# A fp32 encoder trunk on one core: the weights' low parts by an accumulating DMA in place of a VectorE subtraction

## The chip, the cores and the metric

The kernel runs on one NeuronCore of a Trainium2 chip. The core has a matrix engine (TensorE, PE in the profile, with its weight loads as PEld), three engines that work element by element (VectorE, DVE; ScalarE, ACT; GpSimd, POOL), an engine that only issues and waits (SyncE, SP), and 16 DMA engines that all queues share. The metric is the device time of one launch in microseconds. Beside the times stand profiled executions, whose span runs from the first to the last instruction of the program.

## The reference

Two layers of a mixer block work on x of 512 tokens by 1024 channels, in float32. In each layer the normalised input goes through one wide projection; its columns feed a gated convolution module, a bidirectional retention of four heads, and a windowed attention of 16 heads over 4 key heads. Each branch has an output projection, the three are merged by sigmoid gates, and a last projection returns to the residual stream.

```
h = rms_norm(x, norm_g)
z = h @ w_in                                   # 1024 x 14848
...
y_conv = conv_module(...) @ w_conv_out         # 1024 x 1024
y_ret  = retention_branch(...) @ w_ret_out     # 2048 x 1024
y_attn = window_attention_branch(...) @ w_attn_out
g = sigmoid(g_logit + b_gate)
merged = g0 * y_conv + g1 * y_ret + g2 * y_attn
return x + merged @ w_out
```

Every weight is used once per launch, and all 512 tokens are in the core at once.

## The kernel before

**Products in two parts.** TensorE multiplies in a shorter format (float32r) than float32. So each operand is split into a high part, the value rounded to that format, and a low part, the value less the high part, and a product a·b is three matmuls: high·high, high·low and low·high (`mm3`, line 407). An operand's split is `hilo`, a ScalarE copy that rounds and a VectorE subtraction; the weights are split in `weights` (line 387).

**Weights.** The host cuts all matrices into 312 tiles of 128 partitions by 1024 columns (512 KB), 156 for each layer, in the order in which they are used. For each tile SyncE's queue issues a load into `raw` (tag `wraw`), ScalarE writes `wh`, the rounded copy, and VectorE writes `wl`, raw less wh. The tags `wraw`, `wh` and `wl` have three buffers each (`POOLS`, line 27). A buffer of `raw` is free again when `wl` is written, a buffer of `wh` or `wl` when the last matmul that reads it is done.

```
nc.sync.dma_start(out=raw, in_=self.io["wpk"][i])
nc.scalar.copy(out=wh, in_=raw)
nc.vector.tensor_tensor(out=wl, in0=raw, in1=wh.bitcast(F32), op=ALU.subtract)
```

**What uses a tile.** `columns` takes 128 output columns from one tile: eight blocks of 128 rows, three matmuls of 512 tokens each, 24 matmuls into one bank of PSUM (tag `pc`, three banks). `tokens` (line 428) takes four tiles for 512 columns, with tokens on the partitions, in four banks (tag `ps`); each tile feeds 24 matmuls. `tokens256` (line 438) makes a group of four heads' queries from two tiles; for each of four blocks of tokens it goes through all of the first tile and then all of the second (12 matmuls of 256 columns each), so both tiles are held until the last block. There are four such pairs in each layer.

**Order.** The program is first recorded and then put in order by a planner (`Plan`, `order` at line 241), which plays the instructions through with a price for each. Each engine takes, whenever it is free, the most urgent instruction whose operands are there and whose tile has a buffer. Urgency is the place in the program plus an offset; a weight tile's load has the offset -20 us (`LOAD_EARLY`), its split -16 us (`SPLIT_EARLY`), and buffers of one tag are given out in program order. The result is a fixed order on each engine and queue; on the chip an engine that waits holds up what stands behind it. All instructions of the plan are issued from one line, so the profile gives them all line 318 and tells them apart by the tiles' names. The planner's price of a DMA is 60 ns for the queue that issues it, its bytes at 350 GB/s one transfer after the other, and 2 us more until it has landed.

**Stages.** A layer goes through four retention heads (with the convolution's projections and its 31 taps, a VectorE chain in the background, between their steps), then the convolution's layer norm and the keys and values, then the attention, between whose steps gates and projections are set out (`ATT_FILL`), and at the end two projections in sequence (`finish`). GpSimd has little to do before: 62 instructions, memsets, small powers for the norms, and a copy of the attention's sinks into the tiles of the scores.

Of the kernel before, what the change touches and what calls it, by code (L numbers as in the profile page):

```python
# [25 lines left out]
# room, in tiles  # L26
POOLS = {"big": 15, "pp": 8, "mid": 3, "th": 2, "wide": 2, "pads": 1, "wraw": 3, "wh": 3, "wl": 3}
PSUM_POOLS = {"pc": 3, "ps": 4, "ps1": 1}
# planned for: the wait between engines, in ns, and how much longer than its price an instruction takes
LATENCY = 350  # L30
MARGIN = {"vector": 1.06, "scalar": 1.06}
# urgency, in ns
# [3 lines left out]
# the order of the attention's gates (A), merge gates (G), queries (Q) and the convolution's projection (C) between its steps  # L36
ATT_FILL = ["C0", "C1 Q1", "C2", "C3", "C4", "C5 Q2", "C6", "C7", "A0 G0", "Q3 A1", "A2 G1", "A3 G2", "G3", "A4 G4", "A5 G5", "G6", "G7", "A6 A7"]

# columns of the combined input projection
# [4 lines left out]
# columns of the packed parameters  # L44
# [3 lines left out]
# columns of the packed constants  # L48
# [5 lines left out]
class View:  # L54
    """A part of a tile that is allocated when its first instruction is issued.

    ix holds the numbers of the elements that it covers, with the partitions in two halves."""
# [27 lines left out]
    def reshape(self, *shape):  # L85
        """Free dimensions split or joined in order."""
        old = self.ix.shape[1:]
        names = "abcdefgh"
        ix = self.ix.reshape(self.ix.shape[0], *shape)
        fine = len(old) <= len(shape)  # L90
        many, few = (shape, old) if fine else (old, shape)
        groups, i = [], 0
        for n in few:
            g, m = [], 1
            while m < n or (not g):
                m *= many[i]
                g.append(names[i])
                i += 1
            groups.append("(" + " ".join(g) + ")")
        flat = " ".join(names[:len(many)])  # L100
        pat = f"p {' '.join(groups)} -> p {flat}" if fine else f"p {flat} -> p {' '.join(groups)}"
        return self._then("rearrange", (pat, dict(zip(names, many))), ix)
# [42 lines left out]
class Plan:  # L145
    """Records the instructions, orders them, and issues them to Tile in that order.

    Every engine takes, whenever it is free, the most urgent of the instructions whose operands are
    there and whose tiles have room; the engines take turns at a bank of PSUM. Urgency is the place in the program, in ns of the tensor
    engine's work, and an offset. Tiles with one tag are given room in the order of the program, so  # L150
    an order always exists."""
# [16 lines left out]
    def cost(self, engine, method, kw):  # L168
        out = kw.get("out")
        n = out.size if isinstance(out, View) else 0  # L170
        if method == "dma_start":
            return 60
        if engine == "tensor":
            if method == "transpose":
                return 107
            f32 = kw["rhs"].tile.dt == F32
            return max(n, 256 if n > 1 else 64) * (4 if f32 and n > 1 else 1) / 2.4
        src = kw.get("in0", kw.get("in_"))
        psum = isinstance(src, View) and src.tile.tag.pool.psum
        scalars = sum(isinstance(kw.get(k), View) for k in ("scalar", "scalar1", "scalar2", "scale", "bias"))  # L180
        if engine == "scalar":
            return (52 if psum else 94) + 0.833 * n + 93 * (scalars + (kw.get("accum_out") is not None))
        if engine == "gpsimd":
            if kw.get("op") == ALU.pow:
                return 290 + 166 * n
            return 75 + 2.25 * n
        if method in ("bn_stats", "tensor_reduce"):
            n = src.size
        if method == "reciprocal":
            return 62 + 8 * n  # L190
        if method in ("tensor_scalar", "tensor_copy", "memset"):
            n = n or kw["ap"].size
            return 68 + n * (1.042 if psum else 0.521) + 61 * scalars
        if method == "tensor_tensor_reduce":
            return 130 + 1.04 * n
        return 69 + 1.042 * n + 61 * scalars

    def record(self, engine, method, kw):
# [8 lines left out]
        for writes, v in sorted(views, key=lambda x: x[0]):  # L207
            t = v.tile
            tiles[id(t)] = t
            ix = v.ix.ravel()  # L210
            # a start of accumulation clears the whole bank's marks: it comes behind what the bank holds
            seen = t.writer if writes and engine == "tensor" else t.writer[ix]
            deps.update(np.unique(seen).tolist())
            if writes:
                mask = np.zeros(t.writer.size, bool)
                mask[ix] = True
                for r, m in t.readers:
                    if r != number and (m & mask).any():
                        deps.add(r)
                t.writer[ix] = number  # L220
                t.readers = [(r, m) for r, m in t.readers if (m & ~mask).any()]
            else:
                mask = np.zeros(t.writer.size, bool)
                mask[ix] = True
                t.readers.append((number, mask))
# [15 lines left out]
    def order(self):  # L241
# [12 lines left out]
        while len(result) < len(ops):  # L254
# [4 lines left out]
            for e in names:  # L259
# [3 lines left out]
                if free[e] <= t:  # L263
# [15 lines left out]
                    if item is not None:  # L279
# [10 lines left out]
                        if op.method == "dma_start":  # L290
                            n = max(v.size for v in op.args.values() if isinstance(v, View))
                            dma_free = max(dma_free, t) + n * P * 4 / 350
                            op.end = dma_free + 2000
# [39 lines left out]
class Pair:  # L333
    """A [128, 8, 512] array in two tiles of four rows each."""
# [8 lines left out]
class Builder:  # L343
# [43 lines left out]
    def weights(self, key):  # L387
# [7 lines left out]
        with nc.urgency(SPLIT_EARLY):  # L395
            nc.scalar.copy(out=wh, in_=raw)
            nc.vector.tensor_tensor(out=wl, in0=raw, in1=wh.bitcast(F32), op=ALU.subtract)
        return wh, wl

# [4 lines left out]
    def mm3(self, out, a, b, start, stop):  # L404
        """out (+)= (ah + al)^T (bh + bl), without al^T bl."""
        (ah, al), (bh, bl) = a, b
        self.mm(out, ah, bh, start, False)
        self.mm(out, ah, bl, False, False)
        self.mm(out, al, bh, False, stop)

    def columns(self, key, src, pool="pc"):
        """128 columns of src @ w, channels on partitions."""
# [10 lines left out]
    def rows(self, p, t, k, w, c):  # L423
        """adds the part of row k to 128 tokens' columns of src @ w_in."""
# [3 lines left out]
    def tokens(self, col):  # L428
        """512 columns of src @ w_in with tokens on partitions."""
# [8 lines left out]
    def tokens256(self, col):  # L438
        """256 columns of src @ w_in with tokens on partitions, two blocks of tokens in a bank."""
# [20 lines left out]
    def silu2(self, out, p):  # L460
        """2 silu(p) = (1 + tanh(p / 2)) p"""
# [6 lines left out]
    def rstd_of(self, acc, diag):  # L468
        """acc: [128, 512] sums of squares, to be added over the partitions."""
# [41 lines left out]
    def new_input(self, l):  # L511
        """Room for a layer's input, scaled by the norm's gain and split."""
        self.ng = self.gains[:, l * NK:(l + 1) * NK]
        self.uh = self.pair(F32R)
        self.ul = self.pair(F32R)
        self.acc = self.pp()

    def take(self, k):
        """x[k]: x[k] * g split, and its squares into the running sum."""
# [32 lines left out]
    def normalise(self):  # L552
        """h = RMSNorm(x), split."""
# [13 lines left out]
    def derive(self):  # L567
# [6 lines left out]
        # lg[:, 0:4] = log gamma forward; lg[:, 4:8] = -log gamma backward  # L574
# [17 lines left out]
    def toeplitz(self, h):  # L592
        """decay by distance: gamma_f^d for d >= 0, gamma_b^-d for d < 0."""
# [11 lines left out]
    def conv_in(self, c):  # L605
        """a * 2 sigmoid(b) into the padded rows, then the taps in the background."""
# [17 lines left out]
    def queries(self, h, cos, sin):  # L624
        """q, k: channels on partitions; rotary, split."""
# [7 lines left out]
    def values(self, h, first):  # L633
        """v: tokens on partitions; split."""
# [9 lines left out]
    def head(self, h, first):  # L644
# [13 lines left out]
        # scores, transposed: keys on partitions  # L658
# [11 lines left out]
        # gate  # L670
# [3 lines left out]
        # P v  # L674
# [21 lines left out]
        # back to channels on partitions, gated, split  # L696
# [10 lines left out]
        # output projection of two heads  # L707
# [19 lines left out]
    def gate_tanh(self, out, branch, m):  # L727
        """tanh(g / 2) of a merge gate: 2 sigmoid(g) = 1 + tanh(g / 2)"""
# [10 lines left out]
    def conv_stats(self):  # L739
        """y - mean in place, and 1/std spread over the partitions."""  # L740
# [59 lines left out]
    def qk_norm(self, pt, gain):  # L800
        """RMS norm over each head's 64 channels and rotary; tokens on partitions."""
# [29 lines left out]
    def transposes(self, qn, c):  # L831
        """heads 2c and 2c + 1 of four: [128 tokens, (t, h), 64] -> [128, tokens]."""
# [21 lines left out]
    def k_transposes(self):  # L854
        """keys with the channels twice on the partitions, high and low parts."""
# [11 lines left out]
    def q_transposes(self):  # L867
        """queries with the high parts of the channels on the lower partitions, the low parts on the upper."""
# [221 lines left out]
```

## Time and profile before

| | |
|---|---|
| runs | 2034.23 and 2035.17 us, median 2034.7 |
| profiled execution, span | 2032.9 us |
| matmuls and transposes on TensorE | 9436 |
| DMA moved | 184.29 MB, 91 GB/s over the span |
| weight loads | 312 of 512 KB, 3.5 us from issue to landing (median) |
| VectorE's subtractions for the weights | 312, 1222 ns each |
| ScalarE's casts of the weights | 312, 1050 ns each |

The span of the profiled execution is 1.8 us under the median of the runs. In the profile's groups a line names the engine, the operation, what it writes and reads by the tiles' names (`wl<-wraw,wh`), the shapes and the count; behind the bar stand the busy time in microseconds, the mean of one instruction in nanoseconds, and the idle time of the engine just before, with what ended it. A wait stands as who waited, for whom, the total in microseconds, how often, and the longest. A line of the timeline begins with the start and the length of what it merges, in microseconds; "x3" means three instructions in a row. A line of the table by stage begins with a stretch of the span and gives, for each engine, its busy time and its number of instructions, then the granted clock, the busy share of the DMA engines, and GB/s.

### The profile page before, as it was taken

How to read it: one execution, taken by the hardware profiler on the slowest of the kernel's cores; microseconds unless marked ns; L12 is line 12 of the kernel's file. 1: busy time of each engine (PE TensorE's matmuls, PEld its weight loads, DVE VectorE, ACT ScalarE, POOL GpSimd, SP SyncE). 2: the span in 40 equal slices, each digit the busy share in tenths (PEclk: the TensorE clock that was granted, in tenths of full speed). 3: DMA queues.
4: the chain of work that ended last, by engine and by line, in shares of the span. 5: the costliest groups of instructions: out<-in, count | busy, mean ns of one | idle time of the engine just before them, and what ended most of it. 6: DMA issues, size and time to landing. Idle time of an engine off the chain costs nothing.

```text
span 2032.9 us, 24260 instructions
## 1 busy us (share of the span) xinstructions
PE 2021.1 (99%) x9436; PEld 1661.8 (82%) x9436; DVE 1425.8 (70%) x2254; ACT 834.9 (41%) x1361; POOL 56.9 (3%) x62
## 2 busy tenths in 40 slices
PE   8999999999999999999999999999999999999999
PEld 6888888888788888888888888888888888888887
DVE  8788887588575556665567888875885755576652
ACT  5323223233344556673332332232333445566731
POOL 0000000000000000000000000000000000000000
PEclk9999999999999999999999999999999999999999
DMA  5322232222232222223432222222222322222232
GB/s 214 101 73 92 82 94 92 70 86 67 89 94 94 81 75 73 63 82 121 166 99 91 83 92 82 94 93 73 83 73 85 97 88 83 65 82 73 92 106 83
DMA packets 53683, 184.29 MB, mean 91 GB/s; under 512 B 6080, under 2 KB 6336, under 8 KB 53568
## 3 DMA queue, kind: packets, MB, share of 16 engines
q1 hardware_dynamic: 53568, 182.75, 27.9%
q8 instruction: 74, 1.21, 0.2%
q14 instruction: 41, 0.34, 0.0%
HBM read 178.53 MB, written 4.19 MB: 90 GB/s over the span
## 4 chain that ended last, share of the span: by engine, by line
PE 99%; DVE 0%; DMA 0%; issue 0%; ACT 0%; SPq 0%; DVEq 0%
PE pc L318 71%; PE ps L318 29%; DMA big<-xT 0%; DVE wl L318 0%; DVE wide L318 0%; SPq L318 0%; DVE pp L318 0%; ACT pp L318 0%; ACT big L318 0%; DVE sm_m L318 0%; DVEq L318 0%
## 5 line engine op out<-in xcount | busy, mean ns | idle before, releaser
L318 PE MATMUL pc<-big,wh 128*128 128x512 f32 x4096 | 1300.5, 397 | 0.0
L318 PEld LDWEIGHTS pc<-big,wh 128*128 128x128 f32 x4096 | 764.6, 188 | 177.8 <-issue 1.9
L318 PE MATMUL pc<-big,wl 128*128 128x512 f32 x2048 | 811.4, 396 | 0.3 <-DVE wl L318 0.3
L318 ACT CAST wh<-wraw 128x1024 fp32r<-128x1024 f32 x312 | 327.2, 1050 | 800.9 <-PE pc L318 531.9
L318 DVE TENSOR_TENSOR wl<-wraw,wh 128x1024 fp32r<-128x1024 f32 x312 | 380.6, 1222 | 212.0 <-ACT wh L318 210.3
L318 PEld LDWEIGHTS pc<-big,wl 128*128 128x128 f32 x2048 | 384.5, 188 | 91.1 <-DVE wl L318 0.8
L318 DVE SCALAR_TENSOR_TENSOR big<-pads,prm,big 128x512 f32<-128x512 f32 x480 | 340.4, 745 | 1.3
L318 PE MATMUL ps<-wh,big 128*128 128x512 f32 (+1 forms) x1152 | 295.4, 345 | 7.4 <-ACT big L318 7.4
L318 PEld LDWEIGHTS ps<-wh,big 128*128 128x128 f32 x1152 | 200.2, 189 | 35.6 <-ACT big L318 7.4
L318 PE MATMUL ps<-wl,big 128*128 128x512 f32 (+1 forms) x576 | 198.6, 346 | 0.0
L318 PEld LDWEIGHTS ps<-wl,big 128*128 128x128 f32 x576 | 108.9, 189 | 14.6 <-issue 0.5
L318 PE MATMUL ps<-big 128*128 128x512 f32 (+2 forms) x448 | 96.2, 344 | 0.2
L318 PEld LDWEIGHTS ps<-big 128*128 128x128 f32 x448 | 80.7, 188 | 15.6 <-DVE sm_m L318 0.9
L318 PE MATMUL ps<-big,pp 128*128 128x512 f32 x384 | 88.5, 389 | 0.0
L318 PEld LDWEIGHTS ps<-big,pp 128*128 128x128 f32 x384 | 72.1, 188 | 15.3
L318 DVE CUSTOM_DVE_ANT_0 wide<-ps,cst,prm 128x256 f32<-128x256 f32 (+1 forms) x128 | 66.1, 548 | 20.6 <-PE ps L318 19.9
L318 ACT CAST pp<-ps 128x512 fp32r<-128x512 f32 x80 | 46.0, 583 | 74.5 <-PE ps L318 73.9
L318 ACT ACTIVATE wide<-wide,sm_m 128x257 f32<-128x257 f32 (+1 forms) x128 | 70.5, 556 | 6.7 <-DVE sm_m L318 6.7
L318 DVE TENSOR_TENSOR big<-ps,big 64x512 fp32r<-64x512 f32 (+2 forms) x80 | 52.8, 662 | 26.0 <-ACT big L318 20.4
L318 DVE TENSOR_TENSOR pp<-ps,pp 128x512 fp32r<-128x512 f32 x80 | 54.3, 687 | 12.9 <-ACT pp L318 12.5
L318 ACT ACTIVATE wide<-wide,sm_d 128x256 f32<-128x256 f32 (+1 forms) x128 | 62.2, 557 | 2.0 <-DVE sm_d L318 2.0
L318 ACT ACTIVATE big<-mid 128x512 fp32r<-128x512 f32 x64 | 40.0, 630 | 39.0 <-DVE mid L318 39.0
(98 smaller groups left out, 1255.5 us busy)
## 6 DMA issues: line engine op xcount, KB each, us to landing
wraw<-wpk SPq DMA_DIRECT2D x312, 512.0 KB, 3.5
wide<-toe SPq DMA_DIRECT2D x16, 448.0 KB, 3.4
big<-xT SPq DMA_DIRECT2D x8, 256.0 KB, 5.1
pp<-xT SPq DMA_DIRECT2D x8, 256.0 KB, 4.3
xd<-big SPq DMA_DIRECT2D x8, 256.0 KB, 2.0
pp<-xd SPq DMA_DIRECT2D x8, 256.0 KB, 4.5
out<-pp SPq DMA_DIRECT2D x8, 256.0 KB, 2.0
cst<-cst SPq DMA_DIRECT2D x1, 832.0 KB, 7.9
```

The source lines that it names most:

```text
L318: getattr(getattr(self.nc, op.engine), op.method)(**kw)
```

## The change

The low part of a weight tile is no longer a subtraction. ScalarE writes `wl` as raw times -1.0 in the rounded format, which is the high part negated; then GpSimd issues a DMA from `raw` to `wl`, both in SBUF, which adds what it reads to what stands there. The copy to `wh` stays, as do the buffers. The planner is given prices for DMAs of GpSimd's queue: 1100 ns for the issue, twice the transfer time, 3 us until landing. The order of all engines is planned anew with them. The rest of the diff takes comments out.

```diff
@@ cost
         if method == "dma_start":
-            return 60
+            return 1100 if engine == "gpsimd" else 60
@@ order
                             n = max(v.size for v in op.args.values() if isinstance(v, View))
-                            dma_free = max(dma_free, t) + n * P * 4 / 350
-                            op.end = dma_free + 2000
+                            own = e == "gpsimd"
+                            dma_free = max(dma_free, t) + n * P * 4 / 350 * (2 if own else 1)
+                            op.end = dma_free + (3000 if own else 2000)
@@ weights
         with nc.urgency(SPLIT_EARLY):
             nc.scalar.copy(out=wh, in_=raw)
-            nc.vector.tensor_tensor(out=wl, in0=raw, in1=wh.bitcast(F32), op=ALU.subtract)
+            nc.scalar.activation(out=wl, in_=raw, func=AF.Copy, scale=-1.0)
+            nc.gpsimd.dma_start(out=wl, in_=raw, accum_op=ALU.add)
         return wh, wl
```

## The prediction

> **What bounds the kernel now.** I read the page from the top: the busy shares, then the clock and DMA slices, then the chain that ended last, then TensorE's own waits.
>
> ```profile
> span 2032.9 us, 24260 instructions
> PE 2021.1 (99%) x9436; PEld 1661.8 (82%) x9436; DVE 1425.8 (70%) x2254; ACT 834.9 (41%) x1361; POOL 56.9 (3%) x62
> PEclk9999999999999999999999999999999999999999
> q1 hardware_dynamic: 53568, 182.75, 27.9%
> PE 99%; DVE 0%; DMA 0%; issue 0%; ACT 0%; SPq 0%; DVEq 0%
> PE ps L318 <- ACT big L318: 7.4, 1, 7.4
> PE pc L318 <- DVE wl L318: 0.3, 2, 0.2
> ```
>
> TensorE is busy for 2021.1 of 2032.9 us and is 99% of the chain. Of its 11.8 idle us, 7.4 lie before its first matmul, which waits for the first input tile from ScalarE; VectorE's low parts hold it up for 0.3 us in all. A busy PE row can hide a slow pace, so the pace is checked in the chain in order of time:
>
> ```profile
> 919.92 99.87 PE pc L318 x428
> 1043.56 33.60 PE pc L318 x144
> ```
>
> Both give 233.3 ns per matmul (99.87/428, 33.60/144). The table by stage shows what differs around them:
>
> ```profile
> 34.00:310.00 276.00, 276.00 (x1207) 223.58 (x1206) 236.63 (x339) 87.71 (x116) 2.84 (x2) 1.00 0.28 89
> 920.00:1020.00 100.00, 100.00 (x430) 80.60 (x429) 58.25 (x83) 35.89 (x48) 0.00 (x0) 1.00 0.43 139
> 1020.00:1320.00 300.00, 300.00 (x1314) 242.90 (x1313) 249.05 (x358) 93.67 (x124) 4.77 (x3) 1.00 0.28 90
> ```
>
> The third busy figure is VectorE's. It is 58% busy in the second row and 83% in the third, with DMA shares of 0.43 and 0.28, and the pace is the same. So less VectorE work does not quicken a matmul, and more DMA traffic should not slow one. One weight tile feeds 24 matmuls of 512 columns: 24 x 233.3 = 5.60 us.
>
> **The change part by part.**
>
> *VectorE's subtraction goes.* Its rows, with those of the tiles around it:
>
> ```profile
> L318 DVE TENSOR_TENSOR wl<-wraw,wh 128x1024 fp32r<-128x1024 f32 x312 | 380.6, 1222 | 212.0 <-ACT wh L318 210.3
> L318 ACT CAST wh<-wraw 128x1024 fp32r<-128x1024 f32 x312 | 327.2, 1050 | 800.9 <-PE pc L318 531.9
> wraw<-wpk SPq DMA_DIRECT2D x312, 512.0 KB, 3.5
> xd<-big SPq DMA_DIRECT2D x8, 256.0 KB, 2.0
> cst<-cst SPq DMA_DIRECT2D x1, 832.0 KB, 7.9
> ```
>
> 312 x 1.222 us, 380.6 us of VectorE, are taken away. What hides them now is TensorE's unbroken work, so they are worth at most the 0.3 us above.
>
> *ScalarE writes -wh.* The nearest row is its cast of the same tile, 1050 ns. Back to back one costs less; in the last stage of layer 0 a cast and what follows it start 0.95 us apart:
>
> ```profile
> 974.84 1.06 ACT L318 CAST wh<-wraw 128x1024 fp32r<-128x1024 f32 x1 [3.33 <-PE pc L318]
> 980.44 1.06 ACT L318 CAST wh<-wraw 128x1024 fp32r<-128x1024 f32 x1 [3.33 <-PE pc L318]
> 981.39 0.62 ACT L318 ACTIVATE pp<-big 128x512 f32<-128x512 f32 x1
> 986.03 0.63 PE L318 MATMUL pc<-big,wh 128*128 128x512 f32 x2
> 986.50 0.39 PE L318 MATMUL pc<-big,wl 128*128 128x512 f32 x1
> ```
>
> 312 x 0.95 = 296 us put ScalarE at 834.9 + 296 = 1131 us, 56%: not a bound. Behind this write on ScalarE's queue stand evacuations of PSUM, each up to 0.95 us later; three pc banks of 5.6 us each cover that.
>
> *GpSimd issues an accumulating DMA* from SBUF to SBUF, 512 KB, 312 times. No DMA of GpSimd and no accumulating one is in the trace. Call X the time from the end of the write of -wh until TensorE may read wl. Lower end: a store of half the size lands in 2.0 us, and SyncE's issue takes 0.33, so 2.3. Upper end: the 832 KB load that lands in 7.9 us amid the start's traffic, plus an issue as long as GpSimd's longest instruction:
>
> ```profile
> L318 POOL TENSOR_TENSOR qk_r<-qk_v,mhalf 128x16 f32<-128x16 f32 x10 | 29.0, 2901 | 339.2 <-DVE qk_v L318 339.2
> L318 SPq DMA_DIRECT2D wraw<-wpk x312: 327/328/391, 0.7 to 1997.6; - x156
> ```
>
> 7.9 + 2.9 = 10.8. In between: 27.9% of 2032.9 us for 182.75 MB is 1.63 us of all 16 engines per 512 KB (0.524 MB), so a load's 3.5 us hold 1.9 that do not move data. The accumulation reads two tiles and writes one; with the two reads in turn, 3.3 us. With 1.0 for issue (between 0.33 and 2.9, nearer the DMA issue), X = 1.0 + 1.9 + 3.3 = 6.2. I take 6.2.
>
> The Trainium skill has a price of its own: DMA: Bandwidth & Descriptors (Anatomy of one DMA — SWDGE (gpsimd) path) gives a GpSimd DMA about 2.0 us plus its bytes at 436 GB/s, an estimate of X = 4.4 for two reads; by it the body below would lose next to nothing and the kernel would take some 2040 us. No run here shows it yet.
>
> *What the new wait meets.* There are three buffers of wh and wl. In the rows above ScalarE refills a buffer at 974.84, as the tile that used it ends; two tiles later TensorE takes the refilled one, its first wl at 986.50. The two ScalarE writes end 0.95 + 1.05 = 2.0 us after 974.84, so X may be 9.6 us before TensorE waits. I followed the weight tiles from the fourth on (309) from the start of their cast to the first matmul that reads their wl, in program order; the first and the last are
>
> ```profile
> 20.64 2.00 ACT L318 CAST wh<-wraw 128x1024 fp32r<-128x1024 f32 x2
> 27.60 0.39 PE L318 MATMUL ps<-wl,big 128*128 128x512 f32 x1
> 2012.03 1.05 ACT L318 CAST wh<-wraw 128x1024 fp32r<-128x1024 f32 x1 [4.55 <-PE pc L318]
> 2023.73 0.39 PE L318 MATMUL pc<-big,wl 128*128 128x512 f32 x1
> ```
>
> with 7.0 and 11.7 us. Of the 309, 277 have at least 11 us; their cover is the 11.2 us of the two tiles between. 15 have less than 2.0 + 6.2 = 8.2. The structural ones are second tiles of a query projection: tokens256 needs both tiles within 1.4 us:
>
> ```profile
> 678.67 1.05 ACT L318 CAST wh<-wraw 128x1024 fp32r<-128x1024 f32 x1 [1.04 <-PE pc L318]
> 684.31 0.28 PE L318 MATMUL ps<-wh,big 128*128 128x256 f32 x1
> 685.84 0.28 PE L318 MATMUL ps<-wl,big 128*128 128x256 f32 x1
> ```
>
> 685.84 - 678.67 = 7.2 us, 1.0 short. The worst is where a tile is started early, between attention steps:
>
> ```profile
> 812.03 1.04 ACT L318 CAST wh<-wraw 128x1024 fp32r<-128x1024 f32 x1
> 815.18 0.50 PE L318 MATMUL pc<-big,wl 128*128 128x512 f32 x1 [0.16 <-DVE wl L318]
> ```
>
> 3.15 us, 5.1 short. At X = 6.2 all 15 shortfalls add to 29.5 us. Six of them (20.6 us) are such single early matmuls, which the planner places where it expects the weights; it is told of a longer DMA now and can place them later, so I keep the other 8.9 us and 6 of the 20.6, 15 in all.
>
> *The raw tile* is held until the accumulation lands instead of until the subtraction ends: 0.95 + 6.2 - 1.2, some 6 us longer, and SyncE's next load of it, with the loads queued behind, starts that much later.
>
> ```profile
> 955.21 11.53 SPq L318 DMA_DIRECT2D wraw<-wpk  x3
> ```
>
> The last of these three is issued at 955.21 + 11.53 - 0.33 = 966.4 and lands 3.5 later, at 969.9; its cast is the one at 980.44. That cover of 10.5 us still holds, by 4. GpSimd's own small work (62 instructions) is queued among the DMA issues; each waits one issue at most, and none is on the chain.
>
> *The start.* Here nothing is running yet.
>
> ```profile
> 4.47 1.04 ACT L318 CAST wh<-wraw 128x1024 fp32r<-128x1024 f32 x1 [2.45 <-DMA wraw<-wpk]
> 6.57 1.22 DVE L318 TENSOR_TENSOR wl<-wraw,wh 128x1024 fp32r<-128x1024 f32 x1
> 8.80 1.48 PE L318 MATMUL ps<-wl,big 128*128 128x512 f32 x3
> 10.08 1.91 PE L318 MATMUL ps<-wh,big 128*128 128x512 f32 x4
> 0.00:34.00 34.00, 26.64 (x108) 21.49 (x109) 25.86 (x47) 19.65 (x29) 2.32 (x7) 1.00 0.75 274
> ```
>
> Two writes from 4.47 end at 6.5; plus 6.2 makes 12.7 against 8.80, 3.9 later, and the DMA engines are 75% busy there: 5 us.
>
> Sum: 2032.9 + 5 + 15 = 2053 us of span. The median stands 1.8 above the span (2034.7 to 2032.9): 2055 us, 1.0% more. A measurement of this kernel tells about 2% from no change, 41 us.
>
> **Rivals.**
>
> *The accumulation is slower than its buffers allow (slower).* Above X of 9.6 every tile of a dense stage waits, and three buffers turn over in (2.0 + X + 5.6)/3: at 10.8 that is 6.13 instead of 5.60, 0.53 for some 180 tiles with under 12.8 us, 95 us, with some 70 for the short ones and the start: 2200. The 2% are reached earlier, from the short tiles alone: 36 us of body at X = 8.8 if the early six are moved, near 7 if not; at 8.5 with half of them left the body loses 50, 2090. For it: the unseen operation, the upper end of 10.8. Against: the two reads at the rate of the trace.
>
> *The DMA engines run out at the end of each layer.* In 920 to 1020 their share is 0.43, 2.4 us per tile; with 3.3 that is 5.7 of 5.60 us. Two reads at the loads' rate just fit; a third more time per accumulation makes 6.8, 1.2 x 18 tiles x 2 layers = 43 us, 2098. Elsewhere 0.28 leaves room. It decides from about 4 us per accumulation.
>
> *It is hidden almost everywhere:* X near 4.5, the body loses 2, the start 3: 2040. The store's 2.0 us speaks for it.
>
> *A longer price of each stall.* The first matmuls start 0.43 us apart (three from 8.80 to 10.08), later ones 0.23, so TensorE is slow after a pause. In the body no pause as long is shown; if each stall over 3 us brought 3 more us of half pace, the two of 5.1 us would cost 3 us together: 2058. The Trainium skill, TensorE: Matmul & The Clock Gate (What's actually happening), has that rule, an idle window of about 3.4 us halving the clock; the start agrees, the body cannot show it.
>
> *Faster* is bounded by 11.8 us of idle time, 0.6%, most of it ahead of anything this change shortens.
>
> **How the numbers follow.** The forecast (15 in the body, 2045 to 2070) gets 0.42, with the stall price 0.05 beside it; hidden almost everywhere 0.15; X over 8.8 or the six early ones left in place 0.24; the DMA engines 0.12; a gain within 0.6% 0.02. Slower by over 2%: most of the two slow cases, 0.34; within 2%: 0.65; faster by over 2%: 0.01. The range runs from the hidden case less the store's margin, 2036, to X about 9.3 or saturated engines, 2110; that leaves out X above it (0.13) and little below.
>
> **What would show it.** In the profile after: a GpSimd queue of 312 DMAs with time to landing, about 6 us, which is X; ACT near 1131 us and DVE near 1045; TensorE's waits for the landing of wl, in the query projections and before 13 us, not in the dense stages; SyncE waiting for wl's landing instead of VectorE; the pace still 233.3 ns. The prediction is wrong if landings take over 9 us, if TensorE waits in every tile, if matmuls slow beside the new traffic, or if TensorE waits for ScalarE instead.

## The result and the profile after

| | before | after |
|---|---|---|
| median of the runs | 2034.7 us | 2055.67 us (2054.83 to 2056.51) |
| ratio to before, 95% interval | | 1.0103, 1.0086 to 1.012 |
| span of the profiled execution | 2032.9 us | 2053.0 us |

The kernel is 1.0% slower, 20.1 us by the two spans. That is within the 2% that are told from no change, and it is the forecast time. How the 20 us are made up is another matter, and the profile answers it differently from the prediction.

Rows of the changed kernel's page, first. (Line 319 is the line that issues all of the plan, 318 before. The listing ahead of the prediction shows `mm3` at line 404; the text there says 407.)

```profile
PE 2023.3 (99%) x9436; PEld 1661.9 (81%) x9436; DVE 1085.1 (53%) x1942; ACT 1125.1 (55%) x1673; POOL 324.8 (16%) x374
q0 software_dynamic: 44928, 163.60, 44.1%
q1 hardware_dynamic: 53568, 182.75, 28.8%
wraw<-wpk SPq DMA_DIRECT2D x312, 512.0 KB, 4.5
wl<-wraw POOLq DMA_DIRECT2D x312, 512.0 KB, 5.5
xd<-big SPq DMA_DIRECT2D x8, 256.0 KB, 4.5
```

VectorE has 312 instructions and 340.7 us less; ScalarE has 312 instructions and 290.2 us more; a queue of 312 accumulations is new and holds 44.1% of the 16 DMA engines' span, 2.90 us of all 16 for each (0.441 x 2053.0 / 312). A load of the same size takes 1.70 (0.288 x 2053.0 us for 182.75 MB, times 0.524 MB). Nothing here says where TensorE lost time: its busy time rose by 2.2 us only, so 17.9 of the 20.1 us are idle time, and its own waits give it:

```profile
PE ps L319 <- DVE pp L319: 13.5, 1, 13.5
PE ps L319 <- ACT big L319: 7.8, 1, 7.8
PE ps L319 <- DMA wl<-wraw: 3.3, 2, 1.7
PE pc L319 <- ACT wh L319: 0.4, 1, 0.4
PE pc L319 <- DMA wl<-wraw: 0.3, 1, 0.3
```

The 7.8 us before the first matmul were 7.4 before. One wait of 13.5 us is new, and it is not for a weight but for VectorE's `pp`. The landing of `wl` costs 3.3 + 0.3 = 3.6 us in the whole launch. The two waits of 1.7 us lie at 644.6 and 1657.0 us, in query projections.

The table by stage (a stretch; for PE, PEld, DVE, ACT and POOL the busy time and the instructions; granted clock; DMA share; GB/s) puts the new wait in the start:

```profile
0.00:34.00 34.00, 12.76 (x43) 9.81 (x44) 16.61 (x37) 20.03 (x28) 4.49 (x11) 1.00 0.86 273
34.00:310.00 276.00, 276.00 (x1207) 223.37 (x1206) 202.12 (x311) 127.63 (x159) 40.18 (x45) 1.00 0.73 167
930.00:1032.00 102.00, 101.30 (x435) 81.09 (x434) 39.72 (x65) 52.69 (x68) 15.46 (x18) 1.00 0.89 220
```

In the first 34 us TensorE does 43 matmuls where it did 108: 65 x 0.233 = 15.1 us. From 34 to 310 us it is never idle and does 1207, the number of before, although the DMA share rose from 0.28 to 0.73. At the end of layer 0 the DMA engines are 89% busy, and the matmuls keep their pace, as the chain in order of time shows:

```profile
935.55 66.75 PE pc L319 x286
```

66.75/286 is 233.4 ns, at a DMA share of 0.86 over just this stretch (935.55 to 1002.30). The timeline of the start (start and length in us, engine, operation; in brackets the wait before it) shows how the 15 us came about; GpSimd's and VectorE's rows stand behind TensorE's:

```profile
7.77 2.08 PE L319 MATMUL ps<-wh,big 128*128 128x512 f32 x4 [7.77 <-ACT big L319]
23.32 1.86 PE L319 MATMUL ps<-ones,pp 128*128 128x1 f32 x8 [13.47 <-DVE pp L319]
25.04 0.77 PE L319 MATMUL ps<-wl,big 128*128 128x512 f32 x1
25.62 0.63 PE L319 MATMUL ps<-wh,big 128*128 128x512 f32 x1
26.04 0.63 PE L319 MATMUL ps<-wl,big 128*128 128x512 f32 x1
...
6.83 1.04 POOL L319 DMA_DIRECT2D wl<-wraw  x1 [5.92 <-ACT wl L319]
...
18.81 0.37 DVE L319 TENSOR_SCALAR prm<-prm 128x24 f32<-128x24 f32 x2 [3.96 <-DMA prm<-prm]
22.58 0.69 DVE L319 TENSOR_TENSOR pp<-pp,th 128x512 f32<-128x512 f32 x1
```

The first four matmuls that need only `wh` run at 7.77. Before, the first `wl` matmul followed at 8.80. Now ScalarE's write of `wl` ends at 6.5, and the first accumulation is issued at 6.83 and lands at 16.3, 9.5 us later; the tile view of `wl` has this one as its longest:

```profile
DMA to landing us min/median/max: 4.5/5.5/9.5
```

Yet TensorE does not take it at 16.3. The next thing in its queue is the eight sums of the norm (`ps<-ones,pp`), and these need the last of VectorE's squares, which ends at 23.27; VectorE itself stood 3.96 us for the load of the parameters, which landed at 18.8. Only behind the sums, at 25.04, comes the first `wl`. The order of a queue is the planner's. It plays all DMAs one after another, and with the accumulation's doubled transfer its own play-through has the sums at 20.8 us and the first `wl` at 22.2; so it put the sums in front.

X itself I followed tile by tile (309, from the fourth on), from the end of ScalarE's write of the negated high part to the landing: median 5.85 us (4.8 to 7.9 for the middle nine tenths), of which 0.87 is GpSimd's issue (270.8/312). From the landing to the first matmul that reads it the median is 4.1 us.

### The profile page after: what moved, and what is told of

Its sections match the earlier page's. It is cut to its first block, busy times and chain, and to the rows that moved or that the text cites. A ratio compares the mean times of both kernels' runs of the same rounds, so it can differ in the third digit from the quotient of the medians.

```text
span 2053.0 us, 24957 instructions
## 1 busy us (share of the span) xinstructions
PE 2023.3 (99%) x9436; PEld 1661.9 (81%) x9436; DVE 1085.1 (53%) x1942; ACT 1125.1 (55%) x1673; POOL 324.8 (16%) x374
## 3 DMA queue, kind: packets, MB, share of 16 engines
q0 software_dynamic: 44928, 163.60, 44.1%
q1 hardware_dynamic: 53568, 182.75, 28.8%
## 4 chain that ended last, share of the span: by engine, by line
PE 97%; DMA 1%; issue 1%; DVE 0%; ACT 0%; POOLq 0%; ACTq 0%
PE pc L319 68%; PE ps L319 28%; DMA wl<-wraw 1%; DMA wraw<-wpk 0%; DVE wide L319 0%; DVE pp L319 0%; ACT wl L319 0%; POOLq L319 0%; ACT wh L319 0%; DVE sm_m L319 0%; ACTq L319 0%; DVE lg L319 0%
## 5 line engine op out<-in xcount | busy, mean ns | idle before, releaser
L319 POOL DMA_DIRECT2D wl<-wraw x312 | 270.8, 869 | 1533.9 <-ACT wl L319 1397.4
L319 ACT ACTIVATE wl<-wraw 128x1024 fp32r<-128x1024 f32 x312 | 329.2, 1055 | 83.5 <-PE ps L319 83.5
L319 DVE SCALAR_TENSOR_TENSOR big<-pads,prm,big 128x512 f32<-128x512 f32 x480 | 340.7, 747 | 4.4
L319 DVE SCALAR_TENSOR_TENSOR big<-th,pc 128x512 f32<-128x512 f32 x48 | 33.0, 687 | 101.9 <-ACT th L319 101.9
```

Of the source, the lines that this page charges most:

```text
L319: getattr(getattr(self.nc, op.engine), op.method)(**kw)
```

## The experiments

My theory after the result: the start costs some 15 us (a late landing, and an order that put the norm's sums in front), the body some 5. The rival is the prediction's own split, 5 in the start and 15 in the body. A second question is how near the body is to the place where X no longer fits. The ratios are to the kernel before, with 95% intervals.

**Only the first four tiles by VectorE, as before.** In `weights`:

```diff
             nc.scalar.copy(out=wh, in_=raw)
-            nc.scalar.activation(out=wl, in_=raw, func=AF.Copy, scale=-1.0)
-            nc.gpsimd.dma_start(out=wl, in_=raw, accum_op=ALU.add)
+            if i < 4:
+                nc.vector.tensor_tensor(out=wl, in0=raw, in1=wh.bitcast(F32), op=ALU.subtract)
+            else:
+                nc.scalar.activation(out=wl, in_=raw, func=AF.Copy, scale=-1.0)
+                nc.gpsimd.dma_start(out=wl, in_=raw, accum_op=ALU.add)
```

> The first four weight tiles take VectorE's subtraction again, the other 308 the accumulating DMA. Theory A (the loss lies at the start: the profile after has 43 matmuls in the first 34 us where the one before has 108, 65 x 0.233 = 15 us): TensorE's first low part comes near 9 us again, and some 15 of the 20 us come back, 2039 to 2043 us. Theory B (the split of the prediction, 5 at the start and 15 in the body): 5 us come back, about 2050. Theory C (ScalarE's extra writes or the DMA traffic slow the body): nearly nothing comes back, 2053 or more.

Measured: 2041.0 us, ratio 1.0034 (1.002 to 1.0047). Four tiles of 312 return 14.7 of the 21.0 us (2055.67 - 2041.0). The start of this kernel in the table by stage:

```profile
0.00:34.00 34.00, 26.97 (x109) 21.48 (x109) 24.04 (x47) 22.28 (x31) 4.25 (x9) 1.00 0.81 268
```

It does 109 matmuls there, as before. TensorE's waits for the other 308 accumulations:

```profile
PE ps L319 <- DMA wl<-wraw: 3.4, 2, 1.7
PE pc L319 <- DMA wl<-wraw: 2.2, 2, 1.9
```

These are 5.6 us in the body. The prediction's split falls: by it, this kernel would have stood at about 2050.

**Another price for the planner alone.** The instructions are those of the changed kernel; the planner expects an accumulation 6 us after its issue and lets it neither wait for nor delay other transfers. In `order`:

```diff
                             own = e == "gpsimd"
-                            dma_free = max(dma_free, t) + n * P * 4 / 350 * (2 if own else 1)
-                            op.end = dma_free + (3000 if own else 2000)
+                            if own:
+                                op.end = t + 6000
+                            else:
+                                dma_free = max(dma_free, t) + n * P * 4 / 350
+                                op.end = dma_free + 2000
```

> All 312 tiles by the accumulating DMA; only the planner's price of it changes: 6 us after its issue it has landed, and it neither waits for the loads nor delays them. The planner then puts TensorE's first low part ahead of the norm's sums. Theory A1 (half of the start's loss is the order: the first low part has landed at 16.3 us, but TensorE stands behind the norm's sums until 23.3): TensorE goes on near 16 us, 6 to 8 us come back, 2047 to 2050. Theory A2 (the landing is what is late, the order only stands beside it): no change, 2055. Theory B (the body): changes only with the order of the query tiles, within 2 us of 2055.

Measured: 2048.09 us, ratio 1.007 (1.0055 to 1.0085), 7.6 us under the changed kernel. Its start, in the timeline (the line's number moves with each edit):

```profile
16.66 0.80 PE L322 MATMUL ps<-wl,big 128*128 128x512 f32 x1 [7.44 <-DMA wl<-wraw]
```

TensorE now takes `wl` as soon as it lands, at 16.66 instead of 25.04, and does 69 matmuls in 34 us. Of the start's cost about 7.5 us were the order of TensorE's queue and about 7 the late landing, which this order does not shorten. Whether another order of the loads beside it would was not tested.

**Both together.** The first four tiles by VectorE, and the planner's other price (the two diffs above).

> The first four tiles by VectorE's subtraction and the planner's new price for the others. Theory A: the start is that of the kernel before and the body loses at most the 4.5 us of waits that the profile after shows from 34 us on: 2035 to 2041 us. Theory C (a cost of the accumulations in the body): 2045 or more.

Measured: 2039.05 us over ten runs, ratio 1.0024 (1.0014 to 1.0033); span 2038.0, so 5.1 us over before. TensorE's waits:

```profile
PE ps L322 <- DMA wl<-wraw: 3.4, 2, 1.7
PE pc L322 <- DMA wl<-wraw: 1.4, 2, 1.0
```

4.8 us of waits for the landing make nearly all of the 5.1. That is the price of the accumulation in the body. It is the fastest version with the accumulation, and it is still slower than the kernel before.

**ScalarE's write alone.** The kernel before, with the write of the negated high part into `wl` ahead of the subtraction, which overwrites it:

```diff
             nc.scalar.copy(out=wh, in_=raw)
+            nc.scalar.activation(out=wl, in_=raw, func=AF.Copy, scale=-1.0)
             nc.vector.tensor_tensor(out=wl, in0=raw, in1=wh.bitcast(F32), op=ALU.subtract)
```

> The kernel before with ScalarE's write of the negated high part into wl added, which VectorE's subtraction then overwrites; no DMA of GpSimd. Theory A (ScalarE has room and the write costs nothing in the body): 2034 to 2037 us, the 1 to 2 being the first tile's low part, which comes a write later. Theory C (ScalarE's writes delay the evacuations of PSUM that TensorE needs): 2040 or more, with waits of TensorE for ScalarE in the body.

Measured: 2043.8 us, ratio 1.0048 (1.0031 to 1.0065), outside what the first theory gave, and not by the rival's mechanism either. Most of the 9.1 us sit at one place. TensorE's waits, then VectorE's and TensorE's timeline there:

```profile
PE pc L318 <- DVE mid L318: 5.0, 1, 5.0
PE ps L318 <- DVE wl L318: 1.3, 2, 0.6
```

```profile
50.35 1.21 DVE L318 TENSOR_TENSOR wl<-wraw,wh 128x1024 fp32r<-128x1024 f32 x1
52.56 1.22 DVE L318 TENSOR_TENSOR wl<-wraw,wh 128x1024 fp32r<-128x1024 f32 x1 [1.01 <-ACT wl L318]
53.71 1.88 DVE L318 TENSOR_TENSOR mid<-pc,pp 128x512 f32<-128x512 f32 x3
...
55.73 1.19 PE L318 MATMUL pc<-big,wh 128*128 128x512 f32 x2 [5.05 <-DVE mid L318]
56.72 0.63 PE L318 MATMUL pc<-big,wl 128*128 128x512 f32 x1
57.15 1.05 PE L318 MATMUL pc<-big,wh 128*128 128x512 f32 x2
```

The rotary step (`mid<-pc,pp`) frees a `pc` bank, and TensorE waited for the bank. In the kernel before, VectorE does this step between its two subtractions, at 47.67:

```profile
47.67 1.88 DVE L318 TENSOR_TENSOR mid<-pc,pp 128x512 f32<-128x512 f32 x3
51.64 1.22 DVE L318 TENSOR_TENSOR wl<-wraw,wh 128x1024 fp32r<-128x1024 f32 x1 [2.09 <-ACT wh L318]
```

Here the order, planned anew, puts both subtractions in front of it, and the second of them also stands 1.01 us for ScalarE's second write. So the pause comes of the planner's order as well as of ScalarE's write; the two shares were not separated by a run. After the 5.05 us the matmuls stand 0.43 us apart until 60.6, which is another 2.3 us. This joint cost does not exist in the changed kernel, where no subtraction waits. TensorE's other new waits come to 1.3 us, so 288 us more work on ScalarE (1122.5 against 834.9; 296 were forecast) are hidden elsewhere. The two cannot be added to make the changed kernel.

**Two buffers of wl instead of three**, on the changed kernel, and as a control on the kernel before:

```diff
-POOLS = {"big": 15, "pp": 8, "mid": 3, "th": 2, "wide": 2, "pads": 1, "wraw": 3, "wh": 3, "wl": 3}
+POOLS = {"big": 15, "pp": 8, "mid": 3, "th": 2, "wide": 2, "pads": 1, "wraw": 3, "wh": 3, "wl": 2}
```

> The changed kernel with two buffers of wl in place of three. If the cover is the tiles between a buffer's release and its next use, one tile (5.6 us) is left for a write of 1.05 us and the median of 5.85 from its end to the landing: a buffer turns over in 1.05 + 5.85 + 5.6 = 12.5 us, 6.25 for each tile instead of 5.60, on some 220 densely placed tiles 140 us, 2150 to 2260 us with the shorter covers beside them, and TensorE waits for the landing of wl throughout. If the landing is not what a third buffer covers (another limit, or landings that stretch only because there is time), within 30 us of 2055.

> The kernel before with two buffers of wl: the control of the run with two buffers above. VectorE's subtraction of 1.2 us, a hop and 5.6 us of use turn a buffer over in some 7.2 us, 3.6 for each tile: no loss, 2034 to 2040 us. If two buffers by themselves cost time whatever writes the low part, it is slower by 30 us or more.

Measured: the changed kernel 2276.99 us, ratio 1.1194 (1.1171 to 1.1216); the control 2040.73 us, ratio 1.003 (1.0016 to 1.0043). The same buffer is worth 221 us with the accumulation and 6 with the subtraction. TensorE's waits in the first of the two, and GpSimd's timeline in a dense stage:

```profile
PE pc L319 <- DMA wl<-wraw: 51.3, 57, 2.7
PE ps L319 <- DMA wl<-wraw: 34.5, 30, 3.1
PE pc L319 <- ACT wh L319: 30.3, 49, 2.6
```

```profile
57.87 0.86 POOL L319 DMA_DIRECT2D wl<-wraw  x1 [7.25 <-ACT wl L319]
63.78 0.86 POOL L319 DMA_DIRECT2D wl<-wraw  x1 [5.05 <-ACT wl L319]
70.85 0.86 POOL L319 DMA_DIRECT2D wl<-wraw  x1 [6.21 <-ACT wl L319]
```

With two buffers one tile's matmuls must cover the write and X. They don't, and the accumulations follow each other at 6 to 7 us instead of 5.6: the cover works as the prediction described it. The size came out above the expected 2150 to 2260, and part of it is not idle time: TensorE is 72 us busier (2095.3 against 2023.3 us). Some 20 of these are a halved clock (a granted clock of 0.991 over 2275.2 us); the rest was not followed further. The control's 6 us are one wait, again for a bank that VectorE frees late, and half pace behind it:

```profile
PE pc L318 <- DVE mid L318: 3.3, 1, 3.3
```

**A longer X.** Two in-place copies of half a tile by GpSimd stand between ScalarE's write and the accumulation; they leave the values as they are.

```diff
             nc.scalar.activation(out=wl, in_=raw, func=AF.Copy, scale=-1.0)
+            nc.gpsimd.tensor_copy(out=wl[:, 0:512], in_=wl[:, 0:512].bitcast(F32))
+            nc.gpsimd.tensor_copy(out=wl[:, 0:512], in_=wl[:, 0:512].bitcast(F32))
             nc.gpsimd.dma_start(out=wl, in_=raw, accum_op=ALU.add)
```

> The changed kernel with two copies in place by GpSimd of 512 columns of wl (values unchanged) between ScalarE's write and the accumulating DMA, which lengthen the time from the write to the landing by their own length, some 2.4 us, to about 8.3. Theory A (9.6 us is the bound of the dense stages): TensorE still runs through there, and only the short covers lose, 2060 to 2085. Rival (the body has no cover left beyond what the accumulation takes now): 2.4 / 3 = 0.8 us for each of some 220 dense tiles, 176 us, 2200 or more.

Measured: 2126.38 us, ratio 1.045 (1.0429 to 1.0471), between the two. The experiment did two things: the planner saw the copies as well, and its own play-through grew from 1892 to 2023 us with another order on every engine. So I ran the copies again with a planner that gives them no time, which leaves the changed kernel's order as it is. In `order`:

```diff
-                        free[e] = t + op.cost
-                        op.end = t + op.cost + (LATENCY if e != "sync" else 0)
+                        unseen = op.method == "tensor_copy" and e == "gpsimd" and op.args["out"].tile.name == "wl"
+                        free[e] = t + (0 if unseen else op.cost)
+                        op.end = free[e] + (LATENCY if e != "sync" and not unseen else 0)
```

> The two in-place copies by GpSimd once more (0.78 us each, 1.55 together, values unchanged), but the planner is not told of them, so every engine keeps the order of the changed kernel. In the profile after, 14 of 309 tiles have less than 1.55 us between the landing of wl and its first use, 10.3 us short together. Theory A (the landing is covered, and the 70 us of the run with copies that the planner saw came from its other order): 2058 to 2070 us. Rival (that loss is physical, of the later landing itself): about 2126 again.

Measured: 2079.32 us, ratio 1.0219 (1.0189 to 1.0249). X rose by 1.85 us to a median of 7.70, and the time by 23.7 us; the other 47.1 of the 70.7 us were the planner's order. That is above the expected 2058 to 2070. TensorE's waits and VectorE's taps in this kernel:

```profile
PE pc L320 <- DMA wl<-wraw: 9.9, 13, 1.5
PE ps L320 <- DMA wl<-wraw: 9.3, 7, 3.2
```

```profile
L320 DVE SCALAR_TENSOR_TENSOR big<-pads,prm,big 128x512 f32<-128x512 f32 x480 | 378.7, 824 | 4.4
```

TensorE waits 19.2 us for landings, against 3.6. The copies are no pure delay either: VectorE's taps take 824 ns instead of 747.

**Four copies, unseen by the planner** (the same edit with two more copies):

> Four such copies, 3.1 us, unseen by the planner. The landing then comes about 9 us after ScalarE's write, near the 9.6 that the prediction gave as the bound of the dense stages. In the profile after 87 of 309 tiles have less cover than 3.1 us, 76.7 us short together; where neighbours are short one wait serves up to three. Theory A (cover by buffers, as predicted): 2085 to 2135 us, with TensorE's waits all for the landing of wl. Rival (the cover is much larger or smaller than the slack in the profile after): below 2070 or above 2180.

Measured: 2162.44 us, ratio 1.0627 (1.0575 to 1.068), above the expected 2085 to 2135 and below the rival's 2180. X has a median of 9.59, so half of the tiles stand beyond the 9.6 us that the prediction gave as the limit of a dense stage. TensorE's longest waits:

```profile
PE pc L320 <- DMA wl<-wraw: 40.1, 49, 2.2
PE ps L320 <- DMA wl<-wraw: 29.4, 24, 4.8
PE ps L320 <- DVE pp L320: 17.5, 5, 16.1
```

Now 49 waits fall into the projections through `pc` banks, where the changed kernel has one. At 42 of the 49 the tile's own X is above 9.6 us, and at 9 of the 13 with two copies, so the limit shows tile by tile. The three steps of X, 5.85, 7.70 and 9.59, cost the body some 6, 30 and 113 us (2055.67, 2079.32 and 2162.44, each less 2034.7 and the start's 15, though the start's own pause grows too, from 13.5 to 14.0 and 16.1): flat, and then steep near the limit. The copies' load on VectorE has little part in it directly: with four copies TensorE waits 3.1 us for VectorE in all beside the start's 16.1. What it does by way of other engines was not separated.

## Why the prediction was right, and where it was right for the wrong reason

The forecast of 2055 us was met to 0.7 us, and the order of causes behind it was not: the start was mis-sized at 5 us and costs 15, the body was mis-sized at 15 and costs 5. The two errors cancel, so the nearness of the number is luck.

- *VectorE's subtraction was worth nothing.* Held. VectorE lost 340.7 us of work (the forecast DVE time of 1045 is 1085.1, 40 us more, which was not followed up), and TensorE's body gained nothing from it.
- *ScalarE would carry 1131 us and not bound.* Held: 1125.1 us. TensorE waits 0.4 us for `wh`.
- *X of 6.2 us.* Held: 5.85 as a median. The parts are close as well: issue 0.87 (taken as 1.0), 2.90 us of all 16 engines (taken as 3.3, for two reads), and the rest, 2.1 (taken as 1.9). By the Trainium skill, DMA: Bandwidth & Descriptors (Anatomy of one DMA — SWDGE (gpsimd) path), the estimate was 4.4. The trace has 5.85, so here the sum by the traced rows was nearer; the page's figure is near the shortest landing, 4.5 us.
- *Dense stages hold X up to 9.6 us.* Held: no wait between 34 and 310 us at 5.85, and waits in the projections when X is pushed to 9.59. The experiment with two buffers shows the same cover from the other side.
- *The body's 15 us: the step that failed.* The short tiles were taken from the order of before. Followed in the same way, from the start of the cast to the first matmul that reads `wl`, the profile after has 9 of the 309 tiles under 8.2 us, 7.4 us short together, or some 11 with TensorE's waits for them taken off; before had 15 and 29.5. Four of the six early tiles (20.6 us) are placed later, as the prediction thought possible; the worst of them, with 3.15 us before, now has 15.1:

```profile
828.27 1.05 ACT L319 CAST wh<-wraw 128x1024 fp32r<-128x1024 f32 x1 [1.04 <-PE pc L319]
843.40 0.39 PE L319 MATMUL pc<-big,wl 128*128 128x512 f32 x1
```

  The other two belong to the first query projection of each layer. Their first `wl` matmul comes 6.9 us after the cast, 1.7 of it the wait, so their cover is 5.2 us, about that of before (5.3). X is 4.8 us there, and each costs 1.7 us instead of the 3.0 that 6.2 gives. The 8.9 us that the prediction kept do not show: the second tiles of the other query projections, counted at 7.2 us, have 9.6 and more in the new order, and TensorE waits for the landing at no other of the 15 tiles. What is left is the two waits of 1.7 us and one of 0.3: as foretold in kind and place, and 5.1 us with everything in the experiment that isolates the body.
- *The start's 5 us: the other step that failed.* "Two writes from 4.47 end at 6.5; plus 6.2 makes 12.7" took the body's X. Beside the start's loads (DMA share 0.86) the first accumulation took 9.5 us from issue and landed at 16.3, which the upper end of X, 10.8, would have covered. And the sum stopped at the landing. The planner's price put the norm's sums in front of it, and their wait carries TensorE to 23.3. The prediction used the new price for the body ("can place them later") and not for the start.
- *The raw tile held some 6 us longer.* It is hidden: SyncE now waits for the landing, and a load takes 4.5 us instead of 3.5, yet TensorE's waits for `wh` come to 0.4 us.
- *The DMA engines run out at the layers' ends.* It hardly shows: the share is 0.89 at 930 to 1032 us, the pace 233.4 ns, and TensorE waits there for 0.7 us (0.4 for `wh`, 0.3 for `wl`). It is the rival with the least room left.
- *A longer price of each stall.* The mechanism is there, at the start and not in the body. After the 13.5 us the matmuls stand 0.42 us apart (25.62, 26.04), and after the two pauses of 1.7 us the pace is the usual one. The Trainium skill, TensorE: Matmul & The Clock Gate (What's actually happening), names an idle window of about 3.4 us; this start and the 5.05 us pause of ScalarE's write alone agree, and the last section has shorter pauses that were enough.

## What to carry to other kernels

Taking work from an engine that TensorE does not wait for was worth nothing here, although it freed 341 us of VectorE; what counted is the latency of what takes its place against the buffers' cover, and that cover is worked out in tile times (two tiles of 5.6 us here) with its steep end in mind. Work out the start apart: nothing covered it here, the first accumulation took 9.5 us to land beside its loads, and an engine's fixed order can keep it from work that has landed. Where a planner sets the order, a new price for one operation moves everything else, so follow what the planner would do with it at the first tile, and in an experiment hold the order fixed before a delay is read as a delay.

## What the runs showed of the hardware

- An accumulating DMA of 512 KB within SBUF takes 0.87 us to issue, lands 5.5 us after its issue as a median (4.5 to 9.5), and holds 2.90 us of the 16 engines where a load holds 1.7. The other transfers of the changed kernel, beside it, take longer: a load lands in 4.5 instead of 3.5 us, a 256 KB store of `xd` in 4.5 instead of 2.0.
- TensorE's pace does not suffer from DMA traffic of 0.86 of the engines (233.4 ns per matmul, 233.3 before).
- GpSimd's DMA issues leave VectorE's taps alone (747 ns, 745 before), but GpSimd's copies in SBUF do not: 824 ns with two copies a tile and 905 with four. This row is of the last kernel:

```profile
L320 DVE SCALAR_TENSOR_TENSOR big<-pads,prm,big 128x512 f32<-128x512 f32 x480 | 418.0, 905 | 4.4
```

- After pauses TensorE can run at half pace for 3 to 7 us: 0.43 us between matmuls of 512 columns instead of 0.23, and 0.213 instead of 0.117 for 256 columns. The granted clock shows it. In the table by stage, cut at such a spell in the kernel with ScalarE's write alone, it is the 0.50:

```profile
53.72:60.55 6.83, 4.82 (x11) 3.80 (x12) 5.70 (x10) 1.24 (x2) 0.00 (x0) 0.50 0.37 118
```

- No single length of pause divides the cases. Half pace followed pauses of 13.5, 7.4, 5.05 and 3.3 us, of 4.83 and 1.9 us in the kernel with four copies, and of 3.15 us in the one with two; a pause of 3.15 us in the changed kernel with two buffers of `wl` (at 1825.80) was not followed by it. In the eleven profiles the recorded spells, but for the one at the program's end, last 3.41 or 6.83 us, and within a trace they begin whole multiples of 3.41 us apart. Counted in windows of that grid, TensorE was idle for 54.3% or more of the window ahead of 20 of the 22 falls (39 and 48% for the other two), and for 54.2% at most in a window that no fall follows. So what seems to count is the idle share of such a window and not one pause; no run was made to test it.
- The trace after records the clock only from 28.3 us on, and the table by stage shows 1.00 before that as well, so the pace of the start has to be read from the distance of the matmuls.
